# A hybrid RWKV-7/GLA layer on one core: two chunks' outputs moved beside the second triangular solve, and the 64x64 inverse formed once

## The chip, the cores and the metric

The kernel runs on one core of one Trainium2 chip, in one launch. The metric is device time in microseconds (us) of that core; lower is better. The engines spoken of are PE (TensorE, matmuls), DVE (VectorE), ACT (ScalarE), POOL (GpSimd) and SP (the queue that issues nearly all DMAs). Each engine runs its instructions strictly in the order in which they stand in the program.

## The reference, cut to what matters

The model has two layers on 512 tokens of width 1024, batch 1. Layer 0 mixes with RWKV-7 heads and gated linear attention (GLA), layer 1 with differential attention; each is followed by a SwiGLU network of width 2816. The change touches the mixer of layer 0 alone, after its projections:

```
def step(S, inp):                                   # RWKV-7, per head, 64 x 64 state
    r_t, w_t, k_t, v_t, a_t, b_t = inp
    sa = jnp.einsum('bhvk,bhk->bhv', S, a_t)
    S = S * w_t[:, :, None, :] + sa[..., None] * b_t[:, :, None, :] \
        + v_t[..., None] * k_t[:, :, None, :]
    return S, jnp.einsum('bhvk,bhk->bhv', S, r_t)
...
g = jax.nn.sigmoid(xg @ g1) @ g2                    # the RWKV gate, LoRA of width 160
o_a = (y + bonus.reshape(Bsz, T, RW_WIDTH)).astype(h.dtype) * g
...
o_b = o.reshape(Bsz, T, GLA_VW).astype(h.dtype) * jax.nn.silu(gg)   # GLA and its gate
return jnp.concatenate([o_a, o_b], axis=-1) @ w_out
```

## The kernel before, in words

Everything is float32; a large matmul is done as three fp32r matmuls of a high and a low part (`mm3`, L99 to L101). `form_a` streams a weight tile through SBUF, splits it on ACT (`whi`, L88) and DVE (`wlo`, L89) and issues the `mm3`s into one PSUM bank. One such matmul of 128x128 by 128x512 is called a whole matmul below; a projection of 128 outputs is 24 of them.

The recurrence is done in blocks of 64 tokens. The four groups of 128 channels (two heads each) are called chunks 0 to 3. `Chunk` projects keys, receptance and values of one chunk (72 whole matmuls) and `gram` forms its within-block matrices, the last DVE step being L571. Each 64x64 unit lower triangular system is inverted in two steps. `solve` inverts the 32x32 diagonal blocks of two chunks at once by forward substitution: 31 steps of a multiply (L612) and an add (L614), a first solve for chunks 0 and 1 on POOL, a second for chunks 2 and 3 on DVE. A DVE transpose into the table `dg` (L617) and copies (L623) put the blocks on the diagonal of `xd`. `rwkv_out` then applies the inverse as diagonal, below-diagonal block, diagonal again: three products of 128x128 (L640, L647, L654) with copies between them (`z`, `w`). After that come the chunk's transition matrices (L676 into `G`, with `qt`), its offsets (L688), six dependent state steps (L697 on PE, L698 on DVE), the output (L707, L713), its normalisation (L723, L737), and the gate, multiplied out per chunk in plain float32 (L732, L733).

The order of the mixer is: GLA; chunks 0 to 3; the four gate projections of GLA (`gla_gates`, 96 whole matmuls) beside the second solve; then the four `rwkv_out` generators by `interleave` with a lag of five steps, among which the scheduler puts whole matmuls of the output projection as their inputs allow. Of that projection 96 take the GLA half (`ghi`, `glo`) and 96 the RWKV half. A scheduler fixes the order of each engine when the program is built; `high_priority` only shifts that order. The two stages keep their PSUM banks in pools that follow each other, `ps0` and `ps1`.

Of the kernel before, what the change touches and what calls it, by code (L numbers as in the profile page):

```python
# [16 lines left out]
P = 128  # L17
# [408 lines left out]

def gla_gates(g, pool, ob):
    nc = g.nc
    for h in range(4):
        pg = dbank(g)  # L430
        form_a(g, pg, g.ap["win"][16 + h], g.xhi, g.xlo)
        gg = pool.tile([P, T], F32, name="gg", bufs=2)
        nc.vector.tensor_mul(gg, pg, g.rstd)
        nc.scalar.activation(gg, gg, AF.Silu)
        o = pool.tile([P, T], F32, name="o", bufs=2)
        nc.sync.dma_start(o, ob[h])
        nc.gpsimd.tensor_mul(o, o, gg)
        nc.sync.dma_start(ob[h], o)
# [155 lines left out]
def solve(g, st, sp, eng, cs):  # L594


    nc = g.nc
    n = cs[0]
    xl = sp.tile([P, 32, 32], F32, name=f"xl{n}")
    nc.gpsimd.memset(xl, 0.0)  # L600
    nc.gpsimd.memset(xl.rearrange("p t i -> p (t i)")[:, 0::33], 1.0)
    al = sp.tile([P, 32, 32], F32, name=f"al{n}")
    nc.vector.transpose(al.rearrange("p t i -> p (t i)"), st.dg.rearrange("p a c i t -> p t (a c i)"))
    for c in cs:
        for a in range(2):
            nc.gpsimd.memset(st.xd[:, a, c], 0.0)
    buf = sp.tile([P, 256], F32, name=f"tmp{n}")
# [18 lines left out]
def rwkv_out(g, m0, st, sp, c, zeros):  # L626
# [3 lines left out]
    no, G = zeros[c % 2]  # L630
    for e in range(2):
        rows = slice(64 * e, 64 * e + 32)
        nc.scalar.copy(no.rearrange("p (a i) x -> p a i x", a=2)[rows, :, :, 64 * e + 32:64 * e + 64],
                       st.n21[rows, :, c])
    x4 = lambda t: t.rearrange("p (u x) -> p u x", u=4)
    z, w = {}, {}
    for ih in range(2):
        pu = x4(bank(g, use))
# [5 lines left out]
    for ih in range(2):  # L644
        pw = x4(bank(g, use))
        for i in range(4):
            nc.tensor.matmul(pw[:, i], lhsT=no[:, 4 * ih + i], rhs=z[ih][:, i], start=True, stop=True)  # L647
        w[ih] = sp.tile([P, 4, P], F32, name="w", bufs=2)
        nc.vector.tensor_add(w[ih], pw, st.r[:, ih, c])
    yield  # L650
    for ih in range(2):
        pu = x4(bank(g, use))
        for i in range(4):
# [106 lines left out]
def mixer0(g):  # L760
    nc, tc, ap = g.nc, g.tc, g.ap
    with ExitStack() as ctx:
# [40 lines left out]
        st.rt, st.bon, sgd, taild = dram("rt", RC, P, T), dram("bon", RC, P, T), dram("sg", P, T), dram("tail", 32, T)  # L803

        with tc.tile_pool(name="gla", bufs=2) as gp:
            tailw = gp.tile([64, 512], F32, name="tailw", bufs=1)
            nc.sync.dma_start(tailw, ap["tailw"])
            g.rstd, rc = inv_rms_tile(g, square_sums(g, gp, g.xT))
            v = gp.tile([P, 4, 512], F32, name="v", bufs=1)
            for b, pv in enumerate(pvs):  # L810
                nc.scalar.mul(v[:, b], pv, rc[:, b:b + 1])
            m0.th, sg, tail = lora(g, rp, gp)
            nc.sync.dma_start(sgd, sg)
            nc.sync.dma_start(taild, tail[0:32])
            gla(g, m0, gp, v, tail, tailw, ob)

# [10 lines left out]
        nos = [pp.tile([P, 8, P], F32, name=f"no{i}") for i in range(2)]  # L827
        for t in nos:
            nc.gpsimd.memset(t, 0.0)
        left = ExitStack()  # L830
        slv = left.enter_context(tc.tile_pool(name="solve", bufs=1))
        st.dg = slv.tile([P, 2, RC, 4, 32], F32, name="dg")
        nc.gpsimd.memset(st.dg[:, :, 2:], 0.0)
        with tc.tile_pool(name="rwa", bufs=1, side="right") as wk:
# [3 lines left out]
            for c in range(RC):  # L838
# [17 lines left out]
        for x in (first, second):
            for _ in x:
                pass
        right.close()
        psums.close()  # L860
        with ExitStack() as right:
            psum_pool(g, right, "ps1", o0=3, o1=2, pd=3)
            ga = right.enter_context(tc.tile_pool(name="xg", bufs=1, side="right"))
            ghi = ga.tile([P, 4, T], F32R, name="ghi")
            glo = ga.tile([P, 4, T], F32R, name="glo")
            sp = right.enter_context(tc.tile_pool(name="rwb", bufs=1, side="right"))
            st.g2 = sp.tile([P, 512], F32, name="g2")
            nc.sync.dma_start(st.g2, ap["g2"])
            st.tailw = sp.tile([64, 512], F32, name="tailw")
            nc.sync.dma_start(st.tailw, ap["tailw"])  # L870
            st.sg = sp.tile([P, T], F32, name="sg")
# [12 lines left out]
            for h in range(4):
                o = sp.tile([P, T], F32, name="o", tag="part", bufs=2)
                nc.sync.dma_start(o, ob[h])
                nc.scalar.copy(ghi[:, h], o)
                nc.vector.tensor_sub(glo[:, h], o, ghi[:, h].bitcast(F32))
            for j in range(KD):
                pd = dbank(g)  # L890
                form_a(g, pd, ap["wout"][j][:, 512:], ghi, glo)
                t = sp.tile([P, T], F32, name="part", bufs=2)
                nc.scalar.copy(t, pd)
                nc.sync.dma_start(part[j], t)
            for c in range(KD):
                nc.sync.dma_start(g.xT[:, c], ap["xT"][:, c])
            for j in range(KD):
                t = sp.tile([P, T], F32, name="part2", tag="z", bufs=2)
# [3 lines left out]
                form_a(g, pd, ap["wout"][j][:, :512], st.ohi, st.olo)  # L902
# [331 lines left out]
```

## Time and profile before

| | us |
|---|---|
| runs shown: lowest, median, highest of 3 | 1343.78, 1343.85, 1346.37 |
| the profiled execution | 1345.84 |
| its span on the core | 1344.1 |
| PE busy | 1304.0 (97%) |
| DVE busy | 695.9 (52%) |
| ACT busy | 564.6 (42%) |
| POOL busy | 220.5 (16%) |
| granted PE clock, mean of the span | 0.988 |

The profiled execution lies 1.7 us over its span, and 2.0 us over the median of the three runs. The busy time of PE counts overlapping ends of pipelined matmuls, so the distance from one start to the next is the price of a matmul, not its duration. A number in brackets at the end of a timeline row is the idle time of that engine just before, with what ended it. A granted clock of 1.00 is 2.4 GHz, one of 0.50 is 1.2 GHz.

### The profile page before, as it was taken

Reading aid. Unit: us, or ns where it says so; the run is one execution under the profiler, and the core shown is the slowest. Engines: PE = TensorE matmul, PEld = TensorE weight load, DVE = VectorE, ACT = ScalarE, POOL = GpSimd, SP = SyncE. Lnnn points to the kernel's source line nnn. Section 1 sums busy time; section 2 is a strip of 40 time slices with the busy share of each in tenths; the row PEclk is TensorE's granted clock in tenths of the full one; section 3 lists DMA queues with packets and bytes.
Section 4 is the critical chain, followed back from the end, with each engine's and each line's share of the span. In section 5 each row is a group of like instructions: output and inputs, shape, how many; then the busy total and the mean of one; then the engine's idle time right before and its main releaser. Section 6 shows DMA issues by size and latency. Waiting matters only on the chain.

```text
span 1344.1 us, 17769 instructions
## 1 busy us (share of the span) xinstructions
PE 1304.0 (97%) x6868; PEld 1069.9 (80%) x6868; DVE 695.9 (52%) x1185; ACT 564.6 (42%) x953; POOL 220.5 (16%) x209
## 2 busy tenths in 40 slices
PE   8999989799999999999999999999999999999996
PEld 6787767687778888888888888787888888888884
DVE  7475778944553333443344268987634433434332
ACT  5546855443442222222234257776433322223242
POOL 3011193201511110011111000010211100011111
PEclk9999999889999999999999999999999999999998
DMA  6222223423654323433234331220423233333231
GB/s 195 65 70 94 67 70 95 140 72 112 226 158 144 102 71 96 123 94 98 83 88 128 94 86 56 64 63 17 125 86 103 84 84 104 107 104 99 67 99 69
DMA packets 50847, 131.10 MB, mean 98 GB/s; under 512 B 5859, under 2 KB 6243, under 8 KB 50764
## 3 DMA queue, kind: packets, MB, share of 16 engines
q1 hardware_dynamic: 49900, 128.81, 31.5%
q8 instruction: 54, 0.88, 0.3%
q10 hardware_dynamic: 864, 1.17, 0.2%
q14 instruction: 29, 0.24, 0.1%
HBM read 121.22 MB, written 11.36 MB: 99 GB/s over the span
## 4 chain that ended last, share of the span: by engine, by line
PE 89%; DVE 7%; ACT 2%; issue 1%; DMA 0%; DVEq 0%; ACTq 0%
PE pd L101 25%; PE pd L100 25%; PE pd L99 25%; PE po L1033 1%; DVE wlo L89 1%; DVE xl L614 1%; DVE tmp L612 1%; PE sc L1008 1%; PE sc L1009 1%; PE o L697 1%; PE o L101 1%; PE o L99 1%; PE o L100 1%; PE o L654 0%; PE pt L1029 0%
## 5 line engine op out<-in xcount | busy, mean ns | idle before, releaser
L88 ACT CAST whi<-wraw 128x1024 fp32r<-128x1024 f32 (+2 forms) x248 | 215.6, 871 | 533.5 <-PE pd L100 338.8
L101 PE MATMUL pd<-xhi,wlo 128*128 128x512 f32 x1032 | 405.8, 393 | 0.0
L99 PE MATMUL pd<-xhi,whi 128*128 128x512 f32 x1032 | 404.7, 392 | 0.9 <-ACT xhi L180 0.9
L100 PE MATMUL pd<-xlo,whi 128*128 128x512 f32 x1032 | 404.8, 392 | 0.0
L89 DVE TENSOR_TENSOR wlo<-wraw,whi 128x1024 fp32r<-128x1024 f32 (+2 forms) x248 | 259.2, 1047 | 146.7 <-ACT whi L88 146.1
L99 PEld LDWEIGHTS pd<-xhi,whi 128*128 128x128 f32 x1032 | 193.8, 188 | 41.2 <-ACT xhi L180 1.3
L100 PEld LDWEIGHTS pd<-xlo,whi 128*128 128x128 f32 x1032 | 193.9, 188 | 40.3 <-issue 0.2
L101 PEld LDWEIGHTS pd<-xhi,wlo 128*128 128x128 f32 x1032 | 193.9, 188 | 39.6 <-DVE wlo L89 0.2
L215 POOL TENSOR_TENSOR hlo<-h,hhi 128x512 fp32r<-128x512 f32 x44 | 66.8, 1517 | 547.3 <-ACT hhi L214 547.3
L99 PE MATMUL pd<-hhi,whi 128*128 128x512 f32 x352 | 136.9, 389 | 0.0
L100 PE MATMUL pd<-hlo,whi 128*128 128x512 f32 x352 | 136.9, 389 | 0.0
L101 PE MATMUL pd<-hhi,wlo 128*128 128x512 f32 x352 | 136.9, 389 | 0.0
L211 DVE TENSOR_TENSOR ut<-pd,rstd 128x512 f32<-128x512 f32 x44 | 30.4, 692 | 147.0 <-PE pd L101 147.0
L208 DVE TENSOR_TENSOR gt<-pd,rstd 128x512 f32<-128x512 f32 x44 | 30.4, 692 | 124.1 <-PE pd L101 122.0
L99 PEld LDWEIGHTS pd<-hhi,whi 128*128 128x128 f32 x352 | 66.1, 188 | 13.8
L100 PEld LDWEIGHTS pd<-hlo,whi 128*128 128x128 f32 x352 | 66.1, 188 | 13.7
L101 PEld LDWEIGHTS pd<-hhi,wlo 128*128 128x128 f32 x352 | 66.1, 188 | 13.6
L221 DVE TENSOR_TENSOR xT<-pd,xT 128x512 f32<-128x512 f32 x32 | 22.1, 692 | 67.3 <-PE pd L101 67.3
L149 POOL TENSOR_TENSOR ssum<-nsq,ssum 128x512 f32<-128x512 f32 x26 | 38.0, 1460 | 82.2 <-ACT nsq L145 81.8
L1013 ACT ACTIVATE s<-s,mn 128x384 f32<-128x384 f32 (+3 forms) x64 | 35.7, 559 | 21.4 <-DVE mn L1010 20.8
L214 ACT CAST hhi<-h 128x512 fp32r<-128x512 f32 x44 | 27.4, 622 | 37.8 <-DVE h L213 37.8
L989 POOL TENSOR_TENSOR qst<-q,qst 64x512 fp32r<-64x512 f32 x8 | 13.2, 1647 | 167.9 <-DVE qst L987 167.9
(335 smaller groups left out, 1669.1 us busy)
## 6 DMA issues: line engine op xcount, KB each, us to landing
wraw<-in_gate SPq DMA_DIRECT2D x44, 512.0 KB, 3.7
wraw<-in_up SPq DMA_DIRECT2D x44, 512.0 KB, 3.7
wraw<-in_down SPq DMA_DIRECT2D x32, 384.0 KB, 3.1
wraw<-in_win SPq DMA_DIRECT2D x40, 256.0 KB, 2.7
wraw<-in_down SPq DMA_DIRECT2D x32, 320.0 KB, 2.9
wraw<-in_wqk SPq DMA_DIRECT2D x16, 512.0 KB, 3.7
xT<-in_xT SPq DMA_DIRECT2D x16, 256.0 KB, 3.8
wraw<-in_wout SPq DMA_DIRECT2D x16, 256.0 KB, 3.2
```

Source lines behind the costliest of these rows:

```text
L88: nc.scalar.copy(hi, raw)
L89: nc.vector.tensor_sub(lo, raw, hi.bitcast(F32))
L99: nc.tensor.matmul(out, lhsT=lhi, rhs=rhi, start=start, stop=False)
L100: nc.tensor.matmul(out, lhsT=lhi, rhs=rlo, start=False, stop=False)
L101: nc.tensor.matmul(out, lhsT=llo, rhs=rhi, start=False, stop=stop)
L149: (nc.vector if c in fast else nc.gpsimd).tensor_add(ss, sq, first if c == 1 else ss)
L208: nc.vector.tensor_mul(gt, pg, rstd)
L211: nc.vector.tensor_mul(ut, pu, rstd)
L214: nc.scalar.copy(hhi[:, n], h)
L215: nc.gpsimd.tensor_sub(hlo[:, n], h, hhi[:, n].bitcast(F32))
L221: nc.vector.tensor_add(g.xT[:, j], pd, g.xT[:, j])
L1013: nc.scalar.activation(s[:, m, :L], s[:, m, :L], AF.Exp, bias=mn[:, m:m + 1], scale=-1.0, accum_out=sm[:, m:m + 1])
```

## The change

It does four things. The RWKV gate is computed in the GLA stage, as 24 whole matmuls with the high and low parts split (`rwkv_gate`), and goes through DRAM to the end of each chunk; L732 and L733 are gone. `solve` also leaves the transposed diagonal blocks (`xu`), and `below` forms the block below the diagonal of the inverse once, with 32x32 products, so that one product of 128x128 (L697 of the changed file) is left of three. The outputs of chunks 0 and 1 are issued together with the second solve, and the GLA gate projections after them; chunks 2 and 3 follow with a lag of five. The parts of the output projection's input take the place of the layer's own input (`next_acts`), which they can once the gate projections have read it.

```diff
+def rwkv_gate(g, gp, st, sg, tail, tailw):
...
+    for n, x in (("a", g2), ("b", sg), ("c", tailw[0:32]), ("d", tail[0:32])):
...
+        nc.scalar.copy(hi, x)
+        nc.vector.tensor_sub(lo, x, hi.bitcast(F32))
...
+    for c in range(RC):
...
+        mm3(nc, pg, parts[0][:, s], parts[1][:, s], parts[2], parts[3], True, False)
+        mm3(nc, pg, parts[4][:, s], parts[5][:, s], parts[6], parts[7], False, True)
...
+        nc.scalar.copy(t, pg)
+        nc.sync.dma_start(st.gate[c], t)
...
 def gla_gates(g, pool, ob):
...
-        nc.sync.dma_start(ob[h], o)
+    return os
...
-def solve(g, st, sp, eng, cs):
+def solve(g, st, sp, eng, cs, per):
...
+        if s % per == per - 1:
+            yield
...
+    xu = st.xp.tile([P, 32, 32], F32, name="xu", bufs=1)
+    nc.vector.transpose(xu.rearrange("p i u -> p (i u)"), xl.rearrange("p t i -> p i t"))
...
+def below(g, st, sp, c):
...
+                nc.tensor.matmul(pys[0][low, a, i], lhsT=st.n21[top, a, c, i], rhs=st.xu[top, :, a, c, i],
+                                 start=True, stop=True)
+    for e in range(2):
+        low = slice(64 * e + 32, 64 * e + 64)
+        nc.scalar.copy(ya[low], pys[0][low])
...
+                nc.tensor.matmul(pys[1][top, a, i], lhsT=ya[low, a, i], rhs=st.xd[low, a, c, i, low],
+                                 start=True, stop=True)
...
+        (nc.scalar.copy, nc.vector.tensor_copy)[e](st.xd[top, :, c, :, low], pys[1][top])
...
+def rwkv_out(g, m0, st, sp, c, G):
...
+    below(g, st, sp, c)
+    yield
...
-        z[ih] = sp.tile([P, 4, P], F32, name="z", bufs=2)
-        nc.scalar.copy(z[ih], pu)
-    yield
...
-            nc.tensor.matmul(pw[:, i], lhsT=no[:, 4 * ih + i], rhs=z[ih][:, i], start=True, stop=True)
...
-        nc.vector.tensor_add(w[ih], pw, st.r[:, ih, c])
...
-            nc.tensor.matmul(pu[:, i], lhsT=st.xd[:, ih, c, i], rhs=w[ih][:, i], start=True, stop=True)
...
-    nc.tensor.matmul(pg, lhsT=st.g2[:, s], rhs=st.sg, start=True, stop=False)
-    nc.tensor.matmul(pg, lhsT=st.tailw[0:32, s], rhs=st.tail[0:32], start=False, stop=True)
+    gt = sp.tile([P, T], F32, name="gt", bufs=1)
+    nc.sync.dma_start(gt, st.gate[c])
...
+            rwkv_gate(g, gp, st, sg, tail, tailw)
...
-            gla_gates(g, sp, ob)
-        second = solve(g, st, slv, nc.vector, (2, 3))
+        second = solve(g, st, slv, nc.vector, (2, 3), 2)
         next(second)
...
-            interleave([rwkv_out(g, m0, st, sp, c, zeros) for c in range(RC)], 5)
...
+            def take(c):
+                nc.scalar.copy(g.xhi[:, c], ys[c])
+                nc.gpsimd.tensor_sub(g.xlo[:, c], ys[c], g.xhi[:, c].bitcast(F32))
...
+            interleave([second, out(0), out(1)], 0)
+            with tc.tile_pool(name="gates", bufs=1, side="right") as gt:
+                os = gla_gates(g, gt, ob)
+                next_acts(g)
+                for c in range(2):
+                    take(c)
+                for h, o in enumerate(os):
+                    nc.scalar.copy(g.xhi[:, 4 + h], o)
+                    nc.vector.tensor_sub(g.xlo[:, 4 + h], o, g.xhi[:, 4 + h].bitcast(F32))
+            interleave([out(2), out(3)], 5)
+            for c in range(2, 4):
+                take(c)
```

Where instructions moved, first on DVE in the last steps of the second solve. In the kernel before, these are the multiply L612 and the add L614 on the tables `al`, `xl` and `tmp`, with the first half of chunk 0's `G` among the last ones:

```order
L612 TENSOR_TENSOR tmp_2320<-al_2314,xl_2311 128x87
L614 TENSOR_TENSOR xl_2311<-xl_2311,tmp_2320 128x3x29
L612 TENSOR_TENSOR tmp_2320<-al_2314,xl_2311 128x60
L614 TENSOR_TENSOR xl_2311<-xl_2311,tmp_2320 128x2x30
L612 TENSOR_TENSOR tmp_2320<-al_2314,xl_2311 128x31
L681 TENSOR_TENSOR G_2423<-o_2485,dw 64x4x64
L614 TENSOR_TENSOR xl_2311<-xl_2311,tmp_2320 128x31
L681 TENSOR_TENSOR G_2423<-o_2485,dw 64x4x64
L617 STREAM_TRANSPOSE dg<-xl_2311 128x1024
```

Changed, the same table is worked by L644 and L646, and this is the middle of the solve:

```order
L741 TENSOR_TENSOR S<-o_2471,H 128x64
L646 TENSOR_TENSOR xl<-xl,tmp 128x19x13
L644 TENSOR_TENSOR tmp<-al_2182,xl 128x252
L736 COPY S<-H 128x64
L741 TENSOR_TENSOR S<-o_2481,H 128x64
L646 TENSOR_TENSOR xl<-xl,tmp 128x18x14
L741 TENSOR_TENSOR S<-o_2474,H 128x64
L741 TENSOR_TENSOR S<-o_2491,H 128x64
L644 TENSOR_TENSOR tmp<-al_2182,xl 128x255
```

The state steps (L741) of chunks 0 and 1, each of which takes a PE result, now stand between the steps of the solve, one or two of them after a multiply or an add.

On ACT, at the end of the second solve, chunk 2's `below` copies its first product to `ya` (L676) at this place of the changed order (`xd` is printed as `ga`, whose memory it takes; `xhi<-o` are the four gated GLA heads):

```order
L657 COPY ga<-dg 32x2x4x32 x6
L467 ACTIVATE gg<-gg 128x512
L912 CAST xhi<-y 128x512
L922 CAST xhi<-o 128x512 x4
L676 COPY ya<-o_2868 32x256 x2
L685 COPY ga<-o_2869 32x2x4x32
```

The copies to `ya` stand behind the six diagonal copies (L657), the last gate (L467) and five casts (L912, L922); in the kernel before there is no `ya`, and the casts of the heads came after the outputs of all chunks.

On PE, at the end of chunk 3's gram, first the order before (L526 to L582), where `pd` is the bank of a whole matmul:

```order
L526 MATMUL pb<-r,bones 128x512
L550 MATMUL pb<-ar,bkt 128x128 x16
L562 MATMUL pb<-ident,ar 128x128 x4
L566 MATMUL pb<-cst,vs 128x128 x4
L99 MATMUL pd<-xhi,whi 128x512
L100 MATMUL pd<-xlo,whi 128x512
L101 MATMUL pd<-xhi,wlo 128x512
L99 MATMUL pd<-xhi,whi 128x512
L100 MATMUL pd<-xlo,whi 128x512
L576 MATMUL pb<-xT,ga 64x64
L101 MATMUL pd<-xhi,wlo 128x512
L576 MATMUL pb<-xT,ga 64x64 x15
```

The changed order of the same gram (L557 to L613), and what follows it:

```order
L557 MATMUL pb<-r,bones 128x512
L581 MATMUL pb<-ar,bkt 128x128 x16
L593 MATMUL pb<-ident,ar 128x128 x4
L597 MATMUL pb<-cst,vs 128x128 x4
L607 MATMUL pb<-xT,ga 64x64
L613 MATMUL pb<-ident,bkt 128x128 x2
L607 MATMUL pb<-xT,ga 64x64 x15
L613 MATMUL pb<-ident,bkt 128x128 x6
L672 MATMUL o_2215<-xu,n_1059 32x32 x16
L672 MATMUL o_2254<-xu,n_1059 32x32 x16
```

The whole matmuls of the GLA gates that stood inside the gram are gone from it; the gram is followed by the 32x32 products of `below` (L672) for chunks 0 and 1, and the first gate matmuls come behind these.

## Rows read from the trace of the kernel before

**Rows 1.** Busy time by stretch: us, then each engine's, granted clock, DMA share, GB/s.
```profile
130.40:220.80 90.40, 83.72 (x551) 64.06 (x550) 73.19 (x133) 61.93 (x109) 46.08 (x68) 0.98 0.24 77
220.80:282.00 61.20, 50.96 (x484) 45.21 (x484) 49.83 (x112) 29.47 (x54) 10.11 (x10) 0.83 0.35 107
282.00:369.20 87.20, 86.98 (x757) 69.30 (x755) 40.83 (x75) 36.98 (x67) 26.77 (x20) 1.00 0.47 152
```

**Rows 2.** Timeline of PE: start, duration, instruction, idle before it with its releaser.
```profile
184.26 1.89 PE L526 MATMUL pb<-r,bones 128*128 128x512 f32 x2 [3.78 <-DVE r L524]
...
223.78 0.47 PE L99 MATMUL pd<-xhi,whi 128*128 128x512 f32 x1
...
241.35 0.39 PE L101 MATMUL pd<-xhi,wlo 128*128 128x512 f32 x1
248.01 6.06 PE L640 MATMUL o<-r,ga 128*128 128x128 f32 x32 [6.27 <-DVE gg L433]
...
266.79 0.66 PE L697 MATMUL o<-S,G 128*128 128x64 f32 x2 [2.75 <-DVE S L693]
```

**Rows 3.** Busy time in a stretch of 2 us, columns as in the first group.
```profile
278.00:280.00 2.00, 2.00 (x44) 2.00 (x41) 1.26 (x3) 0.44 (x1) 0.00 (x0) 0.50 0.00 0
```

**Rows 4.** Groups by line on DVE, 222 to 262: busy us, mean ns, idle before.
```profile
L614 DVE TENSOR_TENSOR xl<-xl,tmp 128x31 f32<-128x31 f32 (+15 forms) x31 | 13.4, 433 | 0.8
L612 DVE TENSOR_TENSOR tmp<-al,xl 128x31 f32<-128x31 f32 (+15 forms) x31 | 11.6, 374 | 0.8
...
L433 DVE TENSOR_TENSOR gg<-pd,rstd 128x512 f32<-128x512 f32 x4 | 2.7, 683 | 0.0
...
L623 DVE COPY ga<-dg 32x256 f32<-32x256 f32 x2 | 0.7, 384 | 0.0
```

**Rows 5.** Timeline of DVE around the second solve.
```profile
219.61 1.21 DVE L571 TENSOR_TENSOR bkt<-bkt,wc 128x1024 f32<-128x1024 f32 x1
222.18 2.01 DVE L603 STREAM_TRANSPOSE al<-dg 128x1024 f32<-128x1024 f32 x1 [1.37 <-ACT dg L587]
...
235.86 1.36 DVE L614 TENSOR_TENSOR xl<-xl,tmp 128x207 f32<-128x207 f32 x1
...
262.38 1.25 DVE L617 STREAM_TRANSPOSE dg<-xl 128x1024 f32<-128x1024 f32 x1
```

**Rows 6.** Timeline of POOL beside the second solve.
```profile
235.69 1.30 POOL L437 TENSOR_TENSOR o<-o,gg 128x512 f32<-128x512 f32 x1 [3.31 <-ACT gg L434]
```

**Rows 7.** Tiles `G` and `S`, 260 to 330: least/median/greatest ns; idle us, times.
```profile
L681 DVE TENSOR_TENSOR G<-o,dw x16: 405/422/428, 261.4 to 317.1; 64x256 f32<-64x256 f32 x16
...
L698 DVE TENSOR_TENSOR S<-o,H x24: 213/224/225, 267.5 to 326.5; 128x64 f32<-128x64 f32 x24
...
  PE o L697: 18.2, 17
```

**Rows 8.** Timeline of ACT after the second solve.
```profile
262.24 0.62 ACT L887 CAST ghi<-o 128x512 fp32r<-128x512 f32 x1
263.66 3.83 ACT L623 COPY ga<-dg 32x256 f32<-32x256 f32 x6 [0.80 <-DVE dg L617]
```

**Rows 9.** Timeline of PE, outputs of the chunks at the granted clock of 1.00.
```profile
284.13 0.95 PE L723 MATMUL o<-mean,sq 128*128 128x2 f32 x8
284.95 1.10 PE L732 MATMUL o<-sg,g 128*128 128x512 f32 x2
...
287.03 0.43 PE L697 MATMUL o<-S,G 128*128 128x64 f32 x2
287.31 2.00 PE L647 MATMUL o<-z,no 128*128 128x128 f32 x16
...
294.99 0.43 PE L697 MATMUL o<-S,G 128*128 128x64 f32 x2
295.36 1.15 PE L707 MATMUL o<-gr,xT 128*64 128x64 f32 x32
296.44 0.44 PE L713 MATMUL o<-qt,S 64*64 64x64 f32 x6
```

More of the change, by code (lines that the diff above doesn't have):

```diff
@@ L623, in solve @@
             eng(st.xd[rows, :, c, :, 32 * j:32 * j + 32], xt[rows, :, :, c].rearrange("p t a i -> p a i t"))
-def rwkv_out(g, m0, st, sp, c, zeros):
+    xu = st.xp.tile([P, 32, 32], F32, name="xu", bufs=1)
+    nc.vector.transpose(xu.rearrange("p i u -> p (i u)"), xl.rearrange("p t i -> p i t"))
+    st.xu = xu.rearrange("p t (a c i) -> p t a c i", a=2, c=RC)
+def below(g, st, sp, c):
+    nc = g.nc
+    pys = [bank(g, f"o{c % 2}")[:, 0:256].rearrange("p (a i f) -> p a i f", a=2, i=4) for _ in range(2)]
+    ya = sp.tile([P, 2, 4, 32], F32, name="ya", tag="H", bufs=2)
+    for a in range(2):
+        for i in range(4):
+            for e in range(2):
+                top, low = slice(64 * e, 64 * e + 32), slice(64 * e + 32, 64 * e + 64)
+                nc.tensor.matmul(pys[0][low, a, i], lhsT=st.n21[top, a, c, i], rhs=st.xu[top, :, a, c, i],
+                                 start=True, stop=True)
+    for e in range(2):
+        low = slice(64 * e + 32, 64 * e + 64)
+        nc.scalar.copy(ya[low], pys[0][low])
+    for a in range(2):
+        for i in range(4):
+            for e in range(2):
+                top, low = slice(64 * e, 64 * e + 32), slice(64 * e + 32, 64 * e + 64)
+                nc.tensor.matmul(pys[1][top, a, i], lhsT=ya[low, a, i], rhs=st.xd[low, a, c, i, low],
+                                 start=True, stop=True)
+    for e in range(2):
+        top, low = slice(64 * e, 64 * e + 32), slice(64 * e + 32, 64 * e + 64)
+        (nc.scalar.copy, nc.vector.tensor_copy)[e](st.xd[top, :, c, :, low], pys[1][top])
@@ L628, in rwkv_out @@
+def rwkv_out(g, m0, st, sp, c, G):
     nc = g.nc
     use = f"o{c % 2}"
[L630 to L636, printed above, removed]
+    below(g, st, sp, c)
+    yield
     for ih in range(2):
-        pu = x4(bank(g, use))
+        pu = bank(g, use).rearrange("p (u x) -> p u x", u=4)
@@ L826, in mixer0 @@
         st.wc = pp.tile([P, RC, NQ], F32, name="wc")
[L827 to L831, printed above, removed]
+        slv = ctx.enter_context(tc.tile_pool(name="solve", bufs=1))
         st.dg = slv.tile([P, 2, RC, 4, 32], F32, name="dg")
@@ L848, in mixer0 @@
                 if c == 1:
-                    first = solve(g, st, slv, nc.gpsimd, (0, 1))
+                    first = solve(g, st, slv, nc.gpsimd, (0, 1), 31)
                     next(first)
                     next(first)
-        with tc.tile_pool(name="gates", bufs=1, side="right") as sp:
-            gla_gates(g, sp, ob)
-        second = solve(g, st, slv, nc.vector, (2, 3))
+                    next(first)
+        second = solve(g, st, slv, nc.vector, (2, 3), 2)
         next(second)
[L856 to L859, printed above, removed]
+        rps.close()
         psums.close()
@@ L881, in mixer0 @@
-            st.ohi = xo.tile([P, RC, T], F32R, name="ohi")
-            st.olo = xo.tile([P, RC, T], F32R, name="olo")
-            interleave([rwkv_out(g, m0, st, sp, c, zeros) for c in range(RC)], 5)
[L884 to L888, printed above, removed]
+            Gs = []
+            for i in range(2):
+                Gs.append(sp.tile([P, NQ, P], F32, name=f"G{i}"))
+                nc.gpsimd.memset(Gs[i], 0.0)
@@ new lines, in mixer0, with out @@
+            st.xp = sp
+            for _ in first:
+                pass
+            ys = {}
+            def out(c):
+                for y in rwkv_out(g, m0, st, sp, c, Gs[c % 2]):
+                    if y is not None:
+                        ys[c] = y
+                    else:
+                        yield
+            def take(c):
+                nc.scalar.copy(g.xhi[:, c], ys[c])
+                nc.gpsimd.tensor_sub(g.xlo[:, c], ys[c], g.xhi[:, c].bitcast(F32))
+            interleave([second, out(0), out(1)], 0)
@@ new lines, in mixer0 @@
+            with tc.tile_pool(name="gates", bufs=1, side="right") as gt:
+                os = gla_gates(g, gt, ob)
+                next_acts(g)
+                for c in range(2):
+                    take(c)
+                for h, o in enumerate(os):
+                    nc.scalar.copy(g.xhi[:, 4 + h], o)
[3 more added lines that the diff above has]
+                take(c)
@@ L889, in mixer0 @@
+            sp = right.enter_context(tc.tile_pool(name="late", bufs=2, side="right"))
             for j in range(KD):
                 pd = dbank(g)
-                form_a(g, pd, ap["wout"][j][:, 512:], ghi, glo)
-                t = sp.tile([P, T], F32, name="part", bufs=2)
+                form_a(g, pd, ap["wout"][j][:, 512:], g.xhi[:, 4:], g.xlo[:, 4:])
+                t = sp.tile([P, T], F32, name="part")
                 nc.scalar.copy(t, pd)
```

79 lines of the change are left out of this document (31 added, 48 removed).

## The prediction, made before the changed kernel was run

> **What bounds the kernel now.** I read the busy time by stretch first, then the timelines of PE, DVE, ACT and POOL around the second solve, and the groups by line last. PE is busy 97% of the span, so a saving counts where PE is full, and a wait counts where it leaves PE idle. The mixer's second half has three stretches [rows 1]. Up to 220.8 (the end of L571 of chunk 3) PE has 83.7 busy of 90.4 at a granted clock of 0.98. From 220.8 to 282.0 it has 51.0 of 61.2 at 0.83: this is where the second solve runs. From 282.0 to 369.2 it has 87.0 of 87.2 at 1.00, so there each microsecond of PE work is a microsecond of time. In the middle stretch the reader is to see two holes [rows 2]: PE idles 6.27 before L640 at 248.01 and 2.75 before L697 at 266.79, both until DVE is done; behind the first the 32 matmuls of L640 take 6.06, and behind the second the granted clock is still 0.50 (1.2 GHz, instead of 2.4) at 278 [rows 3]. What follows after 369.2 isn't touched.
>
> One price serves throughout: 78 whole matmuls start from 223.78 to 241.35 [rows 2], so each is worth 17.57 / 77 = 0.228. All sums are made on the profiled execution's 1345.84; the median is 2.0 lower. About 0.2%, 2.7 us, is what a measurement of this kernel can tell from no change.
>
> **Leg 1, up to the end of chunk 3's gram.** Added: the gate, 24 whole matmuls in the GLA stage, 24 x 0.228 = 5.5. The four splits on ACT and DVE and the loads of g2 run beside GLA's matmuls, and the four stores of the gate wait for nobody; without that cover a split would cost some 0.7, L433's size [rows 4]. Removed: chunk 3's gram loses the whole matmuls of the GLA gates, which now come later; by the order 12 more whole matmuls stand ahead of its L557 than ahead of L526 before (24 gate, less 12 GLA). If no time of PE was idle for them, that is 12 x 0.228 = 2.7, the low end. The high end adds another 2.7, because the 12 covered DVE's work on r: chunk 2's L526, with little ahead of it, waited 3.78 and then ran slowly [rows 2]. 5.5 + 2.7 = 8.2. I take **+5.5**, halfway, since each of the 12 both costs its place and may be missed as cover.
>
> **Leg 2, from 220.8 (219.61 + 1.21 [rows 5]) until chunk 2's `below` is through its first product.** Before, the like point is 282.0, where the later chunks' L640 starts: 61.2. In the change DVE decides, since the state steps of chunks 0 and 1, their transition matrices and the gates' DVE work all stand between the steps of the second solve, and DVE works strictly in order. Its list:
> - ahead of the solve: `al` 2.0 and the first solve's transposes into `dg` and `xu`, 1.25 each [rows 5], two copies 0.7 [rows 4], a memset of POOL that DVE waits for, 0.8 as an estimate, below POOL's 1.30 for a product [rows 6]: 6.0;
> - 31 steps, 11.6 + 13.4 = 25.0 [rows 4]. In it are four operations that POOL holds up, like the 1.36 of the add at 235.86 [rows 5] beside POOL's product at 235.69 [rows 6], against a mean of about 0.40 [rows 4]: 0.96 each. Now six POOL operations run there (four gated heads, two `take`), so 2 x 0.96 = 1.9 more;
> - between the steps: 7 weight splits, 3 gates and 6 products on `y`, 16 x 0.68 [rows 4] = 10.9; 12 products on `G` and `qt` at 0.42 = 5.0 and 12 state adds at 0.22 = 2.7 [rows 7]; small copies and gaps, an estimate of 3.9 (ten copies at up to 0.38 [rows 4]): 22.5;
> - waits of DVE for PE: between nothing and, for 12 state adds, the 1.07 that one waited before (18.2 in 17 [rows 7]), 12.8; I take 5.0, below the middle, since solve steps stand between them now;
> - the closing transposes, 1.25 twice: 2.5.
>
> That is 62.9. Then ACT, in order: six diagonal copies 3.83, and ahead of `ya` a gate, five casts of 0.62 [rows 8] and `ya` itself, 0.65 twice; 3.83 + 0.62 + 3.1 + 1.3, less 1.25 of the last transpose that runs beside it, 7.6. Together 70.5, **+9.3**. PE's own work in this leg is only about 49 (96 gate matmuls 21.9, the rest the outputs of chunks 0 and 1), so PE isn't the limit and idles some 19. Bounds: without waits, half of the gaps and with the casts elsewhere, 70.5 - 5.0 - 1.9 = 63.6, about +2; with waits twice as long, +15.
>
> POOL's cost is the place where a rule speaks against this change. By the row, a POOL product of 1.30 lengthens one DVE operation by 0.96, since DVE's began 0.17 after POOL's. The Trainium skill, "SBUF — State Buffer", section "SBUF: two separate sides", says that the two engines lock each other out of it for whole instructions when DVE reads two SBUF inputs; the trace agrees. By the rule a DVE operation that begins together with POOL's loses all 1.30, and so do six, 7.8 instead of the 5.8 of the sum.
>
> **Leg 3, from chunk 2's start to the mixer's end,** 87.2 before, PE full. Removed from it:
> - what chunks 0 and 1 still had to do: L723 0.82 and L732 with L733 2.08 (284.13 to 284.95 to 287.03), L737 a quarter of L647's 16, 0.5: 3.4 for chunk 0. For chunk 1 the same and five state steps at 0.37 (294.99 to 295.36), L707 1.08 (to 296.44) and 28 of L713 at the same 0.034 each: 3.4 + 1.9 + 2.0 = 7.3 [rows 9]. 10.7;
> - two of three products of 128x128 for chunks 2 and 3, 4 x 1.98 (L647's 16 at clock 1.00 take 2.00, against 6.06 for 32 behind the hole): 7.9;
> - L732 and L733 of chunks 2 and 3, 2 x 2.08: 4.2;
> - six whole matmuls that the order puts earlier: 1.4.
>
> 24.2. Added: the 32x32 products, 64 records, between nothing and 64 x 0.034 = 2.2 by L707's 32 in 1.08 [rows 9]; I take 1.6, as these are smaller. And 5.0 for a slow clock: PE comes from idle here as it did at 266.79, and then had 0.50 for up to 14 us [rows 2, 3], worth 7; 5.0 allows for a shorter one, with a bound of 0 and one of 9. The gate's load from DRAM is issued some chunks' worth of steps ahead and hidden. 87.2 - 24.2 + 6.6 = 69.6, **-17.6**, bounds -13 and -22.
>
> Sum: 5.5 + 9.3 - 17.6 = -2.8, so 1343.0 for the profiled execution and **1341.0** against the median. Its own range is 1334 to 1346.
>
> **Rivals.** *Faster: PE stays at 2.4 GHz.* If whole matmuls of the gates fill the holes, the clock's 5.0, DVE's 5.0 of waits and POOL's 1.9 all go: -2.8 - 11.9 = -14.7, 1329.1. For it: 1.00 from 282 to 369 while PE is full [rows 1]. Against: the order puts the gates beside DVE's longest list, and PE has too little to fill 70 us. Chance 0.22.
>
> *Slower: the state steps hold the solve.* Before, L698 waited for L697 18.2 us in 17 waits, 1.07 each [rows 7], and nobody stood behind it but the next step. Now each stands ahead of a solve step on DVE. If each of the 12 waits 1.07, 12.8 instead of 5.0, 7.8 more: +5.0, 1348.8. It decides from 0.65 per step, where the 5.0 becomes 7.8 and the gain is gone. For it: DVE's order allows no way round. Against: between two state steps DVE now has solve work that takes as long as PE's part. Chance 0.26.
>
> *POOL blocks wholly.* If all six POOL products begin together with a DVE operation, 2.0 more are lost: -0.8, 1343.0, no change that can be told. For it, the held add ends 0.23 after POOL's product; against, the two engines have no common start. Chance 0.08. The forecast keeps 0.44.
>
> **How the numbers follow.** Faster by over 0.2% (below 1341.2): 0.25 of the forecast's 0.44, all 0.22 of the faster rival, 0.03 of POOL's: 0.50. Within: 0.17 + 0.05 + 0.03 of the slower rival: 0.25. Slower: 0.02 + 0.23 = 0.25. Range 1330 to 1351: it leaves out half of the faster rival (0.11) and the end of the slower one (0.09).
>
> **What would show it.** On DVE the solve's lines (L644, L646) run to about 280 instead of 262 and leave holes that wait for L740; PE idles some 19 us between chunk 3's gram and chunk 2's L672 and shows a clock near 0.5 behind it; on ACT L676 of chunk 2 stands behind L922; L732 and L733 are gone and the mixer ends some 3 earlier than 369.2. If the second solve ends before 270, the faster rival holds; if after 290, with DVE idle before L741, the slower one does; if PE shows no idle there at all, my reading of what bounds leg 2 is wrong, and if leg 3 takes over 75, its removals are.

## The result and the profile after

The changed kernel takes **1353.7 us** in the median of 8 runs (1347.3 to 1355.6), the kernel before 1344.8 beside it: ratio **1.0063, 95% interval 1.0047 to 1.0078**. It is slower; forecast were 1341.0 and 1330 to 1351. The profiled execution is the shortest of the eight, 1347.31 with a span of 1345.5, so it shows 1.5 of the 9 us; what the longer ones add, run e15 shows. Eleven of the kernel's 16 executions on record took 1352.4 to 1359.2, the other five 1346.6 to 1349.9.

Busy time in the prediction's three legs, now (columns as in [rows 1]):

```profile
130.40:236.74 106.34, 90.50 (x566) 68.80 (x564) 76.89 (x141) 62.61 (x108) 45.49 (x70) 0.94 0.22 68
236.74:302.53 65.79, 54.31 (x725) 45.69 (x726) 56.95 (x123) 36.10 (x67) 15.19 (x14) 0.88 0.28 89
302.53:368.91 66.38, 66.19 (x644) 54.90 (x642) 34.80 (x64) 30.48 (x58) 21.43 (x15) 0.99 0.54 168
```

| leg | before | now | moved | forecast |
|---|---|---|---|---|
| 1, to the end of chunk 3's gram | 220.8 | 236.7 | **+15.9** | +5.5 (2.7 to 8.2) |
| 2, to chunk 2's `ya` | 61.2 | 65.8 | +4.6 | +9.3 (2 to 15) |
| 3, to the mixer's end | 87.2 | 66.4 | -20.8 | -17.6 (-13 to -22) |

Together -0.3, and some 1.7 more behind the mixer. Legs 2 and 3 lie within their bounds; leg 1 does not. There the reader is to see 90.5 of 106.3 at a clock of 0.94, where [rows 1] has 83.7 of 90.4 at 0.98. Two terms for what follows: the r product of a chunk is the matmul of `r` with `bones` (L526 before, L557 now), and cover for a wait is work that PE can do in its place. PE's timeline before, the r product of chunk 3 (chunk 2's, with a wait of 3.78, is in [rows 2]):

```profile
214.52 1.10 PE L526 MATMUL pb<-r,bones 128*128 128x512 f32 x2 [1.09 <-DVE r L524]
```

And now, those of chunks 2 and 3:

```profile
197.29 2.05 PE L557 MATMUL pb<-r,bones 128*128 128x512 f32 x2 [4.38 <-DVE r L555]
...
229.04 2.04 PE L557 MATMUL pb<-r,bones 128*128 128x512 f32 x2 [3.87 <-DVE r L555]
```

From 100 to the end of leg 1 the gaps over 0.15 in PE's timeline add up to 14.2, before to 6.1: +8.1. Stretches at 0.50 cost 6.8 there (2-us slices, each times one less its clock), before 1.7: +5.1. The trace counts 624 whole matmuls ahead of chunk 3's r product, before 612: 12 x 0.228 = 2.7. 8.1 + 5.1 + 2.7 = 15.9. That it comes out to the tenth is chance, for the gate's 24 matmuls, of which 12 use 32 rows of the array and not 128, take 7.1 by their starts and not 24 x 0.228 = 5.5.

Of the 8.1 of waits, 2.8 are chunk 3's r product and 0.6 chunk 2's. Most of the rest are new waits of PE for ACT, of 0.6 to 1.1: three for `sig` and two for `sq`. Those for `sig` can be followed. Ahead of it ACT loads a table (ACT_TABLE_LOAD, 1.28). Now ACT stands idle until PE's L492 is through and only then loads, and PE waits for `sig`; here in chunk 0, ACT's timeline and then PE's:

```profile
136.37 1.28 ACT L494 ACT_TABLE_LOAD   x1 [3.33 <-PE pb L492]
```

```profile
138.41 1.73 PE L581 MATMUL pb<-ar,bkt 64*128 64x128 f32 x16 [0.99 <-ACT sig L494]
```

Before, and in run e8 below, which has the gate back at the chunks' ends, the same load starts 0.02 behind ACT's previous instruction, beside PE's matmuls; in e8:

```profile
132.43 0.72 ACT L514 ACTIVATE d<-p,omr 128x512 f32<-128x512 f32 x1
133.17 1.28 ACT L494 ACT_TABLE_LOAD   x1
```

Every profile here with the gate in the GLA stage has two or three such waits, of 0.4 to 1.2; every one with the gate at the chunks' ends has a single one, of 0.32. What in the program's order makes ACT's load wait isn't shown.

Leg 2, DVE's groups from 236 to 297 (columns as in [rows 4]), then ACT's timeline:

```profile
L646 DVE TENSOR_TENSOR xl<-xl,tmp 128x31 f32<-128x31 f32 (+15 forms) x31 | 13.7, 441 | 0.7
L644 DVE TENSOR_TENSOR tmp<-al,xl 128x31 f32<-128x31 f32 (+15 forms) x31 | 11.5, 372 | 0.7
...
L659 DVE STREAM_TRANSPOSE xu<-xl 128x1024 f32<-128x1024 f32 x2 | 3.8, 1913 | 0.0
...
L741 DVE TENSOR_TENSOR S<-o,H 128x64 f32<-128x64 f32 x12 | 2.7, 224 | 1.5 <-PE o L740 1.1
```

```profile
294.73 3.79 ACT L657 COPY ga<-dg 32x256 f32<-32x256 f32 x6 [2.70 <-DVE dg L651]
298.54 0.63 ACT L467 ACTIVATE gg<-gg 128x512 f32<-128x512 f32 x1
299.07 0.60 ACT L912 CAST xhi<-y 128x512 fp32r<-128x512 f32 x1
299.58 2.17 ACT L922 CAST xhi<-o 128x512 fp32r<-128x512 f32 x4
301.78 0.75 ACT L676 COPY ya<-o 32x256 f32<-32x256 f32 x2
```

The 31 steps take 25.2 (forecast 25.0), the 12 state adds waited for PE 1.1 in all, not 5.0 or 12.8, and `ya` stands behind copies, gate and casts as foreseen.

### The profile page after: what moved, and what is told of

Read it like the earlier page. It is cut to its first block, busy times and chain, and to the rows that moved or that the text cites. A ratio compares the mean times of both kernels' runs of the same rounds, so it can differ in the third digit from the quotient of the medians.

```text
span 1345.5 us, 18023 instructions
## 1 busy us (share of the span) xinstructions
PE 1294.2 (96%) x7004; PEld 1059.1 (79%) x7004; DVE 700.6 (52%) x1187; ACT 566.9 (42%) x959; POOL 221.4 (16%) x207
## 4 chain that ended last, share of the span: by engine, by line
PE 73%; DVE 4%; ACT 2%; DMA 1%; issue 1%; POOL 0%; SPq 0%; DVEq 0%; ACTq 0%; POOLq 0%
PE pd L104 22%; PE pd L105 22%; PE pd L106 22%; PE po L1072 1%; PE sc L1047 1%; PE sc L1048 1%; DVE wlo L94 1%; DVE xl L646 1%; PE pt L1068 0%; DMA wraw<-in_gate 0%; ACT whi L93 0%; DMA wraw<-in_up 0%; PE o L740 0%; DMA part<-part 0%; PE o L750 0%
## 5 line engine op out<-in xcount | busy, mean ns | idle before, releaser
L104 PE MATMUL pd<-xhi,whi 128*128 128x512 f32 x1064 | 419.9, 395 | 2.6 <-ACT xhi L922 1.7
L106 PE MATMUL pd<-xhi,wlo 128*128 128x512 f32 x1064 | 420.2, 395 | 0.0
L105 PE MATMUL pd<-xlo,whi 128*128 128x512 f32 x1064 | 419.4, 394 | 0.6 <-DVE xlo L186 0.6
L104 PEld LDWEIGHTS pd<-xhi,whi 128*128 128x128 f32 x1064 | 200.9, 189 | 45.5 <-ACT xhi L922 1.8
L105 PEld LDWEIGHTS pd<-xlo,whi 128*128 128x128 f32 x1064 | 200.6, 188 | 43.0 <-DVE xlo L186 1.9
L106 PEld LDWEIGHTS pd<-xhi,wlo 128*128 128x128 f32 x1064 | 200.8, 189 | 40.7 <-DVE wlo L94 0.2
L1052 ACT ACTIVATE s<-s,mn 128x384 f32<-128x384 f32 (+3 forms) x64 | 35.7, 559 | 21.4 <-DVE mn L1049 20.8
```

Of the source, the lines that this page charges most:

```text
L104: nc.tensor.matmul(out, lhsT=lhi, rhs=rhi, start=start, stop=False)
L105: nc.tensor.matmul(out, lhsT=lhi, rhs=rlo, start=False, stop=False)
L106: nc.tensor.matmul(out, lhsT=llo, rhs=rhi, start=False, stop=stop)
L1052: nc.scalar.activation(s[:, m, :L], s[:, m, :L], AF.Exp, bias=mn[:, m:m + 1], scale=-1.0, accum_out=sm[:, m:m + 1])
```

## The experiments

All but e13 and e15, which are single executions, were timed beside the kernel before (median 1343.4 to 1343.7). "Low" is a stretch of 2-us slices whose granted clock is below 0.97.

**The changed kernel again (e1, e13, e15).** No edit.

> The changed kernel again. Its one profile lost 15.9 us up to the end of chunk 3's gram (236.7 instead of 220.8) and won 16.8 from chunk 2's start to the mixer's end, so its mixer ended where it did before; but its median lies 6.4 us over that profiled execution. Theory: the 6 us are more time at a granted clock of 0.50 behind PE's idle stretches in the mixer (before 197, before 229, before 296), of a length that differs from run to run: a slower execution shows a mixer that ends 4 to 7 us later than 369 and a mean granted clock near 0.981. Rival: the 6 us are lost behind the mixer, in the attention layer or the SwiGLU networks; then the mixer ends at 369 in a slower execution too. Time 1352 to 1355.

> The changed kernel again, for a profile of a slower execution (1353 to 1356). Theory: such an execution has one or two more stretches at a granted clock of 0.50 between 95 and 310 than the profiled ones at 1347, each of about 1.7 us lost or a multiple, and the mixer ends 4 to 7 later than 369. Rival: the mixer ends at 369 and the loss is in the layers behind.

> As e13: a second chance for a profile of a slower execution; between 1347 and 1356, with the mixer's end later than 369 by what the time is above 1347.

e1: 1353.97, ratio 1.0076 (1.0053 to 1.0100), its profiled execution again a short one, 1347.0. e13: 1346.6. e15: 1357.8, a longer execution. The same stretch of the GLA stage in the first profile of the changed kernel, then in e15:

```profile
96.00:112.00 16.00, 16.00 (x114) 12.49 (x115) 2.82 (x8) 7.21 (x15) 0.00 (x0) 1.00 0.30 115
```

```profile
96.00:112.00 16.00, 16.00 (x74) 12.21 (x73) 1.73 (x4) 4.42 (x8) 0.00 (x0) 0.57 0.21 82
```

PE is busy all 16 us in both; at 0.57 it gets 74 matmuls through instead of 114, a loss of 6.8. What it does there, in e15's timeline of PE:

```profile
97.02 0.44 PE L106 MATMUL pd<-dhi,clo 32*128 32x512 f32 x1
97.39 0.79 PE L104 MATMUL pd<-bhi,ahi 128*128 128x512 f32 x1
97.98 0.63 PE L105 MATMUL pd<-blo,ahi 128*128 128x512 f32 x1
98.41 0.63 PE L106 MATMUL pd<-bhi,alo 128*128 128x512 f32 x1
98.97 0.79 PE L104 MATMUL pd<-dhi,chi 32*128 32x512 f32 x1
```

These are the gate's matmuls, three on 128 rows of the array and three on 32 in turn, the clock falling at about 97.3 behind the first narrow three. GLA's small products stand between them, in both executions. e15 reaches the end of leg 1 at 242.8, 6.1 later than the first profile, and its mixer's last matmul starts at 377.04 instead of 368.52. So e1's theory is right on the place, as far as one longer execution can show: of e15's 10.5 us 8.5 are lost in the mixer, and about 6 of them before leg 1 ends. It is wrong on the cause, for the largest fall doesn't stand behind an idle stretch of PE. (A loss of 1.7 at 380 lies behind the mixer.) The short executions e1 and e13 aren't free of it either: their clock fell for 3.4 at 110, some 1.5 behind the gate's last matmul, with PE busy; e13:

```profile
110.00:114.00 4.00, 4.00 (x14) 2.98 (x15) 0.78 (x3) 0.26 (x1) 0.00 (x0) 0.58 0.37 137
```

**The gate alone (e2).** The kernel before with `rwkv_gate` of the changed one:

```diff
             gla(g, m0, gp, v, tail, tailw, ob)
+            rwkv_gate(g, gp, st, sg, tail, tailw)
...
-    nc.tensor.matmul(pg, lhsT=st.g2[:, s], rhs=st.sg, start=True, stop=False)
-    nc.tensor.matmul(pg, lhsT=st.tailw[0:32, s], rhs=st.tail[0:32], start=False, stop=True)
+    nc.sync.dma_start(gt, st.gate[c])
```

> The kernel before with the RWKV gate alone moved into the GLA stage. Theory: the loss up to chunk 3's gram comes with the gate's 24 matmuls, which take the place of projection matmuls there, so chunks 0 to 2 reach their r product (L526 before at 130.5, 152.0, 184.3) 4, 11 and 13 us later, as in the changed kernel; the GLA gates stay as cover in chunk 3, so there it is about 10 later than before; 8.3 are saved behind (L732, L733 four times 2.08). Time 1345 to 1349. Rival: the loss comes from taking the GLA gates out of chunk 3's gram and from the new order of DVE, and the gate costs its 24 x 0.228 = 5.5 and no more: chunks 1 to 3 5.5 later, time 1340 to 1343.

1350.5, 1.0055 (1.0041 to 1.0069). The r products come at 140.5, 168.8, 203.6 and 235.1, low from 100 to 112 for a loss of 5.1, PE again busy 16.00 of the 16 us from 96. They are 10 to 21 later than before, where the theory had 4 to 13, and the median lies above its range; the profile is the longest of the six executions (1354.5). The gate's move alone makes the kernel slower, by 6.9.

**The gate undone (e4, e8).** The changed kernel with L732 and L733 at the chunks' ends again:

```diff
-            rwkv_gate(g, gp, st, sg, tail, tailw)
...
+    nc.tensor.matmul(pg, lhsT=st.g2[:, s], rhs=st.sg, start=True, stop=False)
+    nc.tensor.matmul(pg, lhsT=st.tailw[0:32, s], rhs=st.tail[0:32], start=False, stop=True)
```

> The changed kernel with the RWKV gate put back to the end of each chunk in plain float32 (order and inverse as changed). Theory (the gate's place costs most of the loss up to chunk 3): chunk 3's r product comes at 217 to 221 instead of 229, the end of the mixer gets 8.3 back: 1349 to 1352, a few us less than the changed kernel. Rival (the GLA gates taken out of chunk 3's gram cost it): chunk 3's r product only 5.5 earlier, 8.3 more at the end, some 3 slower than the changed kernel: 1354 to 1358.

1352.4, but spoilt: `sg` and `tail` lay in a table of the first solve, their loads waited on SP for it, and with them the weights behind; PE waited 11.88 at 218. With these two loads on POOL's queue:

```diff
-            nc.sync.dma_start(st.sg, sgd)
+            nc.gpsimd.dma_start(st.sg, sgd)
```

> The changed kernel with the gate back at the end of each chunk in plain float32, and the two tables of the gate now loaded from POOL's queue: in the run before this one they waited on SP for the first solve and held up the weights behind them, PE idle 11.88. Theory (the gate's place costs most of the loss up to chunk 3): chunk 3's r product at 215 to 217 instead of 229, 8.3 us more in the outputs: 1346 to 1350. Rival (the GLA gates taken out of chunk 3's gram and the new order cost it): r product at 220 to 223, 1352 to 1356.

**1339.2, 0.9964 (0.9951 to 0.9978): faster than before**, by more than the theory said. PE's timeline:

```profile
215.71 2.04 PE L557 MATMUL pb<-r,bones 128*128 128x512 f32 x2 [3.81 <-DVE r L555]
...
360.93 0.39 PE L106 MATMUL o<-xhi,wlo 128*128 128x512 f32 x1
```

Leg 1 ends at 223.8, 12.9 earlier than in the changed profile: 24 matmuls less (600 against 624) are 5.5 at 0.228 each, gaps of 9.1 instead of 14.2 are 5.1, slow clock of 5.1 instead of 6.8 is 1.7. The two matmuls per chunk that are back cost only 4.7 in leg 3 (71.1 instead of 66.4) and 0.7 in leg 2 (66.5 against 65.8): there PE wasn't the limit. The wait of chunk 3's r product is still 3.81, so that one comes with the order, not with the gate.

**Narrow or not (e6, e11).** The 32-row half is padded with zeros to 128 rows, in the changed kernel (e6) and in e2 (e11); as many matmuls, in the same place:

```diff
+        if k < P:
+            nc.vector.tensor_sub(hi, sg, sg)
+            nc.vector.tensor_sub(lo, sg, sg)
```

> The changed kernel with the gate's narrow half (32 rows of the array) padded with zeros to 128 rows, in the same place. Theory that the narrow matmuls let the clock fall: the dips between 95 and 115 go and the median comes down by 2 to 3 us (1350 to 1352). Rival: the dips come from what surrounds them (GLA's small products without projections between), so nothing changes beyond noise: 1352 to 1355.

> The kernel before with the gate alone moved into the GLA stage, its 32-row half padded to 128 rows (unpadded it was 1350.5, at 0.50 from 100 to 112 in its profile). Theory: no dip between 95 and 115, 1346 to 1348; the rest of the loss is 24 matmuls and displaced order. Rival: padding changes nothing here, 1349 to 1352.

e6: 1348.7, 1.0039 (1.0026 to 1.0052), 5 below the unpadded kernel. e11: 1348.1, 1.0028 (1.0019 to 1.0037), against 1350.5. The stretch of above in e6:

```profile
96.00:112.00 16.00, 16.00 (x122) 13.98 (x122) 2.78 (x7) 8.79 (x17) 0.00 (x0) 1.00 0.27 103
```

122 matmuls at 1.00; e11 has 124 at 1.00 there. With the padding the fall is gone, and so are the long executions: of e6's five none took over 1350.1, of e11's eleven none over 1349.7. Two things differ besides. Padded, the 24 take 6.0 by their starts, 7.1 unpadded at 1.00, where a matmul starts 0.32 behind one of the other height (96.57 to 96.89) and 0.23 behind one of its own; and a GLA product at 87.5 waits 0.9. Neither is of the size of the 5. In e11 the r products come at 134.4, 162.7, 197.0 and 228.8: without the fall they are the 4, 11 and 13 later that e2's theory had for chunks 0 to 2.

**The gate ahead of GLA (e5, and padded e9).**

```diff
-            gla(g, m0, gp, v, tail, tailw, ob)
             rwkv_gate(g, gp, st, sg, tail, tailw)
+            gla(g, m0, gp, v, tail, tailw, ob)
```

> The changed kernel with the RWKV gate's 24 matmuls issued ahead of GLA's own work instead of behind it, so that projection matmuls stand again among GLA's small products. Theory (the gate among GLA's small products lets the granted clock fall between 95 and 145, and displaces the projections that filled the gaps): no stretch below 0.97 from 95 to 150, chunk 0's r product at 136 with 457 whole matmuls ahead of it, chunk 1's at about 160; median 3 to 5 us below the changed kernel's 1354, 1349 to 1351. Rival (24 matmuls more are 24 matmuls more, wherever they stand, and the dips of the clock belong to PE's idle stretches in the chunks): chunk 3's r product stays at 229 and the median at 1352 to 1355.

> The gate ahead of GLA again (the run of that was at 0.50 from 64 to 82, behind a hole of PE of 4 us, while 128-row and 32-row matmuls took turns), now with the 32-row half padded with zeros to 128 rows. Theory (turns of narrow matmuls hold the clock at its lower level): the hole stays, but the clock is back at 1.00 some 4 us behind it, by 70 instead of 82; median 6 us lower than that run's 1357, about 1350. Rival (the clock stays low for as long as the hole's consequences last, whatever the shape): low until 80 again, 1355 to 1358.

e5 missed: 1357.0, 1.0101 (1.0087 to 1.0116). PE now waits for the gate's splits and is then low from 64 to 82, a loss of 8.5:

```profile
59.59 1.98 PE L337 MATMUL pb<-tail,tailw 16*128 16x512 f32 x4
63.90 1.80 PE L104 MATMUL pd<-bhi,ahi 128*128 128x512 f32 x4 [2.34 <-ACT bhi L441]
65.51 0.63 PE L105 MATMUL pd<-blo,ahi 128*128 128x512 f32 x1
65.93 0.63 PE L106 MATMUL pd<-bhi,alo 128*128 128x512 f32 x1
66.49 0.79 PE L104 MATMUL pd<-dhi,chi 32*128 32x512 f32 x1
```

e9, padded, is low from 62 to 70 only (a loss of 3.4), as expected, and its mixer ends at 376.0, 5.6 ahead of e5's 381.6. But its median is 1355.9, 1.0082 (1.0068 to 1.0096), not 1350. The forecast took 6 from 1357.0, e5's median, while e5's profile is its longest execution, 1359.6; and e9's profile loses 1.3 more than e5's to a low clock behind the mixer. The shape's effect on the clock is seen again; between the medians it is 1.2, and why it isn't more stays open.

**The inverse alone (e3, e7, e14).** The kernel before with `below` and one product for three. Where the first solve's `xu` is transposed was decided by memory in e3 (it lay where the gated heads had been; PE waited 13.97) and by the scheduler in e7 (it came ahead of chunk 2's gram on DVE, which then waited for POOL's solve). The edit, then e7's wait on DVE:

```diff
-    no, G = zeros[c % 2]
+    below(g, st, sp, c)
...
-            nc.tensor.matmul(pw[:, i], lhsT=no[:, 4 * ih + i], rhs=z[ih][:, i], start=True, stop=True)
```

```profile
208.12 1.90 DVE L625 STREAM_TRANSPOSE xu<-xl 128x1024 f32<-128x1024 f32 x1 [18.94 <-POOL xl L614]
```

> The kernel before with the inverse formed once as the only change: one product of 128x128 for each chunk half instead of three, 32x32 products in their place, order and gate as before. Theory: 16 products of 128x128 for two matmuls each, 4 x 2 x 1.98 = 15.8 us of PE's work, go, 4 x 3.2 = 12.8 of 32x32 products would come back if none overlapped; by the changed trace 64 records take 2.0 for two chunks and 1.2 for two more, so some 6 in all: 6 to 10 us faster, 1334 to 1339. Rival: DVE's two further transposes (1.9 each) and the copies between stand on the path behind the second solve, where PE waits, and lengthen its idle stretch and the slow clock behind it by as much: 1342 to 1346.

> The kernel before with the inverse formed once as the only change, and now with the transposed blocks (xu) in memory of their own: in the run before this one they lay where the gated heads had been, and PE waited 13.97 for that. Theory: PE's idle stretch behind the second solve is again 6 to 8 us, two of three products go, 16 x 1.98 / 2 = 15.8 us, against 6 for the 32x32 products: 1334 to 1340. Rival: what is taken away stood beside waits of the outputs for DVE and ACT (state steps, copies), so PE idles or its clock stays at 0.50 for it: 1341 to 1346.

e3 1348.9 and e7 1365.2 tell only that. e14 gives `xu` a write that needs chunk 3's gram, and so the place that the changed order has:

```diff
+    if cs[0] == 0:
+        nc.scalar.copy(xu[0:32, 0, 0:1], st.n21[0:32, 0, 3, 0, 0:1])
```

> The kernel before with the inverse formed once alone; the first solve's xu is transposed right behind chunk 3's gram. Theory A (the inverse makes the gain, the order none): two of three products gone, 4 x 2 x 1.98 = 15.8 us of PE, less some 6 for the 32x32 products: 1334 to 1340. Theory B (the order makes it: what is taken away here stood beside waits and slow clock that stay): 1341 to 1346.

1345.1, 1.0011 (1.0002 to 1.0020): no gain; theory B. PE's waits in its timeline:

```profile
247.23 2.02 PE L640 MATMUL o<-xu,n 32*32 32x32 f32 x64 [5.43 <-DVE gg L433]
251.85 1.45 PE L649 MATMUL o<-ga,ya 32*32 32x32 f32 x32 [2.61 <-ACT ya L644]
256.31 3.79 PE L665 MATMUL o<-r,ga 128*128 128x128 f32 x16 [3.01 <-DVE ga L653]
...
267.95 1.45 PE L649 MATMUL o<-ga,ya 32*32 32x32 f32 x32 [4.60 <-ACT ya L644]
```

15.7 of waits, where before the same stretch has 9.8 (6.27 and 2.75 in [rows 2], and one of 0.73): in the old order PE has nothing ready between the 32x32 products and the copies behind them, and much of the removed work comes back as waiting, with 1.7 more of low clock. (This profile is the shortest of e14's executions, 1342.0.) With the new order besides (e8) the kernel is 5.9 faster. The order without the inverse wasn't tried.

**Cover for chunk 3, then for chunk 2 (e10, e12).** e8 with the first GLA gate projection issued ahead of chunk 3's gram; in e12 a second ahead of chunk 2's:

```diff
+                if c == 3:
+                    o0 = slv.tile([P, T], F32, name="o0")
+                    nc.sync.dma_start(o0, ob[0])
+                    one_gate(g, wk, o0, 0)
                 ch[c].gram()
```

> The changed order and inverse with the gate back at the chunks' ends (the run of that was 1339.2), and the first of the four GLA gate projections, 24 matmuls, issued ahead of chunk 3's gram again: 12 stand before its r product, 12 inside the gram. Theory (lost cover: PE waits 3.81 before the r product and 1.32 inside the gram, with 3.4 of slow clock behind): the wait falls to about 1, the dip from 214 to 222 goes, the 24 matmuls are missing later where PE was full: 3 to 5 us faster than 1339, 1334 to 1336. Rival (the 24 matmuls were the cover of the second solve, where PE now gets its holes): 1338 to 1341.

> The kernel of the run before this one (1336.1: gate at the chunks' ends, one GLA gate projection ahead of chunk 3's gram) with a second GLA gate projection ahead of chunk 2's gram: 18 whole matmuls more stand before chunk 2's r product, where PE waited 3.78 and ran at 0.50 for 3.4 behind it. Theory (PE's waits for r are lost time that any ready matmul fills): that wait is under 0.5 and the dip at 186 goes, chunk 3's r product comes at most 1 us later than 215.4 although 24 more matmuls stand ahead of it: 3 to 5 us faster, 1331 to 1333. Rival (DVE's and ACT's work for the added gate lengthens the chain to r, and the second solve, now with 48 gate matmuls beside it, leaves PE a longer hole): no faster than 1336, 1335 to 1339.

e10: **1336.1, 0.9941 (0.9929 to 0.9953)**, the fastest of all; the wait is 1.09 as it was before the change, and the low stretch at 214 is gone:

```profile
215.37 1.10 PE L563 MATMUL pb<-r,bones 128*128 128x512 f32 x2 [1.09 <-DVE r L561]
...
357.44 0.39 PE L106 MATMUL o<-xhi,wlo 128*128 128x512 f32 x1
```

e12 missed by far: 1349.6, 1.0042 (1.0031 to 1.0053).

```profile
189.33 2.04 PE L563 MATMUL pb<-r,bones 128*128 128x512 f32 x2 [3.98 <-DVE r L561]
```

Chunk 2's r product comes 4.2 later than in e10 (185.12), the length of the 18 matmuls (18 x 0.228 = 4.1), and the wait is as long as before. The added projection was through at 178.3, where DVE takes its result, ahead of the receptance's last matmuls. What runs ahead of those delays the chain to r and fills nothing; only what runs between the last of them and the r product is cover. Most of e12's loss lies elsewhere, though: its mixer ends 14.0 later than e10's (371.9 against 357.8), and up to there low stretches cost it 18.8 instead of 8.5. The longest begins at 236.7, behind a wait of 2.77, and lasts 17.1.

## Why the prediction was wrong

- **The step that failed is leg 1**, the gate's move: +5.5, that is "24 x 0.228 = 5.5", with 2.7 and 8.2 as its bounds. Measured: +15.9 in a short execution, +22.0 in e15. The count and the lost cover were right: 12 more matmuls stand ahead of chunk 3's r product, and its wait grew by 2.8, the high end's other 2.7. The 24 were priced as whole matmuls, though 12 have 32 rows, and took 7.1. Left out were two terms. *The waits*, 5.3 more: PE's waits for ACT's `sig` and `sq` in each chunk, which come with the gate's move (e8 has none over 0.4), and a longer one for chunk 2's r. The 24, ahead of the projections, cover none of these; e12 shows the same of another projection. *The clock*: leg 1 had no term of its own for it. There it cost 5.1 more, behind PE's waits, and in the longer execution another 6.8 between 96 and 112, where PE doesn't wait.
- Leg 2 was overpriced by 4.7, within its bounds: the solve's 25.0 was right, the state adds' waits for PE (5.0) were 1.1, as solve steps now stand between them; `xu`'s transposes take 1.9 each, not 1.25. PE was idle 11.5 of the leg, not some 19. It waited 5.45 for `xu` at 296.5, and the clock was low from 293.9 to 304.1, as expected.
- Leg 3's removals came: -20.8 against -17.6. But of the 8.3 on L732 and L733 only 5.4 is time by e8: 4.7 in leg 3, and 0.7 in leg 2, where those of chunks 0 and 1 stand and PE isn't the limit.
- The faster rival didn't come (0.88 in leg 2). The slower rival had the sign right and the cause wrong: the state adds hold nothing. POOL's rival was right on the single case and wrong on the number of them: a step of about 0.2, begun 0.05 behind a POOL operation of 1.26 at 292.1, took 1.26, but only four of the 62 operations met one (1.25 to 1.5), and all took 25.2 instead of the 26.9 of the sum.
- What the change's parts are worth: the gate's move 14.5 (1339.2 of e8 to 1353.7), the inverse alone +1.4, order and inverse -4.4. They don't add up: in the old order the gate's move costs 6.9 (e2), in the new 14.5, and the runs don't show what makes up all of the difference. The median lies 2.7 above the range; no rival had the gate at fault.

## What to carry to other kernels

Work that is cheap by count can be dear by place: price a moved matmul by what waits behind it, and ask of each wait whether the work added runs before or after the last input of the chain that it is meant to cover. Before a wait is filled, look whether PE's shape there is wide; here matmuls on 32 rows, back to back with wider ones, ran at half the clock in some executions and not in others, so that one profile may not show it. Where a change has several parts, undo one at a time: here the order and the inverse together won 4.4 and the gate's move lost 14.5, and the fastest kernel keeps the two, drops the third and puts one GLA gate projection back as cover.

## What was not expected of the hardware

The granted clock fell to 0.50 with PE never idle: 16.00 busy of 16 us, while three matmuls on 32 rows took turns with three on 128, among GLA's small products, in e2 and e15; in e1 and e13 it fell right behind the gate's last matmuls, for 3.4. It didn't in every execution of the same program (1.00 from 96 to 112 in the first profile of the changed kernel), nor there in the two profiles with the 32 rows padded in place or in any with the gate at the chunks' ends. In e5 the same turns stayed at 0.50 for 17.1 behind a wait of 2.34, in e9, padded, for 6.8 behind the same wait. The Trainium skill, "TensorE: Matmul & The Clock Gate", section "Part 1: The HAM clock gate", puts the lower level down to PE's idling; the falls behind PE's holes (idle 5.45 before 296.5, low from 293.9) agree, this one doesn't, and the measurement decides. That the shape is the cause rests on e6 and e11, in time and in the trace; that the zeros' values play no part wasn't tested, nor the change between two shapes apart from the narrow one, nor the turns without GLA's small products, except behind e5's wait.
